# The fixed order of TensorE's work in a hybrid backbone's first mixer, set anew

## The chip, the cores and the metric

The kernel runs on one core of one Trainium2 chip, in one launch, with float32 inputs and output. The metric is device time in microseconds (us): the median of the runs shown. A profiled execution is taken beside them, from which the rows in this document come.

## What is computed

The program computes two layers of a diffusion backbone over 512 latent tokens and 256 context tokens, 1024 wide. The part that matters here is the mixer of layer 0. One input projection gives queries, keys, values and output gates of gated linear attention (GLA, 4 heads), a low-rank `z` from which its forget gates come, and queries, keys and values of ordinary attention:

```python
gq, gk, gv, gog, gz, aq, ak, av = _split(h @ w_in, EVEN_SIZES)
for d, z in enumerate(jnp.split(gz, 2, axis=-1)):
    logit = z @ gla_w_gate[d] + gla_b_gate[d]
    g = jax.nn.log_sigmoid(logit) / GLA_GATE_TAU
    # S_t = diag(exp(g_t)) S_{t-1} + k_t v_t^T,  o_t = S_t^T q_t, in both directions
```

The context is scanned alone, and the latent tokens start from its last state. Every sub-layer is also shifted, scaled and gated by vectors of a modulation, `silu(c) @ mod_w + mod_b`, for the latent tokens and for the context.

## The kernel before, in words

Tokens are kept in six tiles of 128 (0 to 3 latent, 4 and 5 context). A projection's float32 product is made of three matrix products of parts: weights and activations are split into a high and a low part (`wH`, `wL`), and `mm3` (L496) adds high by high, high by low and low by high. A weight unit is loaded by SyncE into `raw` (three buffers), cast by ScalarE to `wH` (L484), and what is left is put by VectorE into `wL` (L485); there are four buffers of each. "nat" products have tokens on the partitions and work two token tiles at a time in a two-bank PSUM tile (`mm_tile`, two buffers): 48 matmuls of 256 columns, called a block below. Queries and keys of GLA (`gqk`) come transposed, in groups of 512 and of 256 tokens. PSUM's eight banks are shared out as two two-bank tiles (`mm`), two single ones that `sc_tile` hands out in turn (`sc0`, `sc1`), and two of `tr_tile` (`tr`).

`even_mixer` (L825) first makes `z` (nat products of 288 columns), turns it (`zTp` to `zT`, L868 to L874) and then makes all of the forget factors in `gla_gates` (L982): for each of two head pairs, the context and the latent tokens, and two directions, one matmul gives `logit`, in bank `sc1` each time. ScalarE takes the absolute value, exponential, logarithm (L995 to L997), VectorE the minimum and the difference (L998, L999), ScalarE the last exponential into `glaf` (L1000).

After that, TensorE's order is written out by hand. Each word in the strings that `run` takes (L961 on) advances a generator by one step, and while `pinned` is set, TensorE's instructions stay in that program order. The other engines' order is chosen by a scheduler when the program is built, and is fixed from then on. The words are: `qk0`, `qk1` (GLA's queries and keys of a head pair), `v0`, `v1` (values), `g0`, `g1` (output gates), `q`, `kv` (ordinary attention's), `p` (its preparation, no matmuls), `m` (a step of the modulation), and `c0`, `l0`, `c1`, `l1`, the scans of head pair 0 and 1 over the context and the latent tokens.

A step `m` (`mod_vec`, L318) loads 512 KB of `mod_w` into `mraw` (three buffers in the pool `gate`) and lets VectorE add it to two accumulators `macc` (L340, L342). After eight steps TensorE sums over the partitions (`mod_acc`), VectorE copies the rows (`modrows`, L279), TensorE turns them (`modT`), and, for one of the two modulations here, turns a gate row (`gcT`). Both modulations end before the pool `gate` is given back (`tp.release()`), and the pool of the scans is opened in its place.

A scan (`scan`, L659) has six steps: (1) multiply queries and keys by decays in levels of 1, 2, 4 tokens, each level copied by ScalarE (`qkg`, L733) and then multiplied by VectorE (L738); (2) small score products of these levels (`pcg`, 32 by 32, into `sc` banks), and the levels 8 to 64; (3) `pcg` of the levels 8 and 16; (4) `pbg`, the scores of 32 and 64, and the keys turned (`knpg`, `tr` banks), which ScalarE copies (`kng`, L785); (5) the chunk states' products (`pdg`, in an `sc` bank, L794), and the chain of states on VectorE (`Sg`, L803, L805); (6) the outputs (`pog`, `tr` banks). The masked parts of `pcg` are taken out of the bank by ScalarE and VectorE (`CTg`, L717, L720).

## Time and profile before

| what | value |
|---|---|
| median of 3 runs | 1807.64 us (1806.29 to 1809.88) |
| the profiled execution's own time | 1812.69 us |
| its span, first to last instruction | 1810.8 us |
| mean granted TensorE clock | 0.975 |
| the mixer's `z` products end, attention's first transposes begin | 58.5 us, 293.0 us |

In rows of the timeline the columns are start, duration, engine, line, operation, output <- inputs, shape, count, and in brackets the idle time before and what ended it. In rows of a window table they are the stretch, its length, the busy time of TensorE, its weight loads, VectorE, ScalarE and GpSimd with counts, the granted TensorE clock (1.00 is full), and the DMA share and rate; a table for one tile has fewer columns. In grouped rows the count is followed by the busy time, the mean of one in ns, and the idle time before with its causes.

### The profile page before, as it was taken

The page shows a single profiled execution, that of the slowest core. Times are in us where ns is not written, and L with a number is a line of the kernel's source. Part 1 is how long each engine was busy: PE and PEld are TensorE (multiplying, and loading weights), DVE is VectorE, ACT ScalarE, POOL GpSimd, SP SyncE. Part 2 cuts the span into 40 slices and gives each one's busy share as a digit, 9 for nine tenths or more (in the row PEclk, how much of TensorE's full clock was granted, in tenths as well). Part 3 has the DMA queues.
Part 4 walks back from the last instruction along what each step waited for, and adds up shares of the span by engine and source line. Part 5 has one row for each costly group of instructions (what it writes and reads, how often), then busy time and mean ns, then how long its engine had stood idle before and what let it go on. Part 6 is the DMA issues. An engine that isn't in the chain of part 4 may idle for free. (4 is left out here: it accounts for less than half of the span.)

```text
span 1810.8 us, 33217 instructions
## 1 busy us (share of the span) xinstructions
PE 1728.3 (95%) x13864; PEld 1547.5 (85%) x13864; DVE 1299.4 (72%) x2095; ACT 877.4 (48%) x1562; POOL 59.1 (3%) x73
## 2 busy tenths in 40 slices
PE   6699888999999999999999999999999999999998
PEld 4488886787898888989899898888998899999997
DVE  5855485875596999888667715778875487878875
ACT  5526464764644333323334825666564464434442
POOL 1001020000000000000000100000000000000000
PEclk8699888999999999999999999999999999999999
DMA  8632103004433546454124412211114333333333
GB/s 312 189 100 59 42 21 102 21 2 151 140 111 87 152 144 195 149 165 139 58 63 149 140 47 71 60 48 53 55 48 129 110 100 99 111 94 94 94 106 127
DMA packets 169587, 187.28 MB, mean 103 GB/s; under 512 B 6198, under 2 KB 140892, under 8 KB 169436
## 3 DMA queue, kind: packets, MB, share of 16 engines
q1 hardware_dynamic: 167504, 181.56, 32.3%
q10 hardware_dynamic: 1932, 3.59, 0.6%
q8 instruction: 109, 1.79, 0.4%
q14 instruction: 42, 0.34, 0.1%
HBM read 175.66 MB, written 9.46 MB: 102 GB/s over the span
## 5 line engine op out<-in xcount | busy, mean ns | idle before, releaser
L485 DVE TENSOR_TENSOR wL<-raw,wH 128x1024 fp32r<-128x1024 f32 (+1 forms) x126 | 151.4, 1208 | 134.8 <-ACT wH L484 134.5
L165 PE MATMUL nat<-wH,x 128*128 128x256 f32 (+1 forms) x1216 | 230.5, 289 | 0.5 <-issue 0.5
L539 ACT CAST wH<-raw 128x1024 fp32r<-128x1024 f32 x120 | 124.6, 1052 | 177.7 <-PE acc L165 102.8
L165 PEld LDWEIGHTS nat<-wH,x 128*128 128x128 f32 x1216 | 195.1, 195 | 2.2 <-issue 1.1
L484 ACT CAST wH<-raw 128x1024 fp32r<-128x1024 f32 (+1 forms) x126 | 128.9, 1038 | 131.4 <-PE nat L165 37.9
L540 DVE TENSOR_TENSOR wL<-raw,wH 128x1024 fp32r<-128x1024 f32 x120 | 145.3, 1221 | 63.0 <-ACT wH L539 62.8
L165 PE MATMUL nat<-wL,x 128*128 128x256 f32 (+1 forms) x608 | 174.6, 287 | 0.0
L165 PE MATMUL acc<-wH,gH 128*128 128x512 f32 x440 | 172.6, 393 | 0.0
L165 PE MATMUL acc<-wH,gL 128*128 128x512 f32 x440 | 171.7, 390 | 0.0
L165 PE MATMUL acc<-wL,gH 128*128 128x512 f32 x440 | 171.5, 390 | 0.0
L632 DVE TENSOR_TENSOR y<-y,acc 128x1024 f32<-128x1024 f32 x135 | 114.8, 862 | 30.6 <-PE acc L165 27.3
L165 PE MATMUL ff<-x,wH 128*128 128x512 f32 (+1 forms) x512 | 127.6, 340 | 0.0
L342 DVE SCALAR_TENSOR_TENSOR macc<-mraw,scT,macc 128x1024 f32<-128x1024 f32 x98 | 122.9, 1279 | 6.3 <-DMA mraw<-in_mod_w_dram 6.2
L165 PEld LDWEIGHTS nat<-wL,x 128*128 128x128 f32 x608 | 118.6, 195 | 0.2 <-DVE wL L485 0.2
L412 POOL TENSOR_TENSOR rs<-ms,neghalf 128x1 f32<-128x1 f32 (+2 forms) x62 | 57.1, 923 | 1734.5 <-DVE ms L410 1734.5
L165 PE MATMUL oproj<-wH,x 128*128 128x512 f32 x320 | 102.8, 398 | 3.1 <-ACT x L453 3.0
L165 PEld LDWEIGHTS acc<-wH,gH 128*128 128x128 f32 x440 | 82.6, 188 | 19.8 <-issue 2.5
L165 PEld LDWEIGHTS acc<-wH,gL 128*128 128x128 f32 x440 | 82.6, 188 | 17.4
L165 PEld LDWEIGHTS acc<-wL,gH 128*128 128x128 f32 x440 | 82.7, 188 | 16.1
L165 PEld LDWEIGHTS ff<-x,wH 128*128 128x128 f32 x512 | 87.3, 190 | 10.0
L733 ACT COPY qkh<-arr 128x512 f32<-128x512 f32 x112 | 70.2, 642 | 36.3 <-DVE arr L738 32.1
L165 PE MATMUL ff<-x,wL 128*128 128x256 f32 (+1 forms) x256 | 86.2, 337 | 0.0
(329 smaller groups left out, 4134.4 us busy)
## 6 DMA issues: line engine op xcount, KB each, us to landing
mraw<-in_mod_w_dram SPq DMA_DIRECT2D x96, 512.0 KB, 4.5
raw<-in_ffn_w_gate_dram SPq DMA_DIRECT2D x44, 512.0 KB, 4.1
raw<-in_ffn_w_up_dram SPq DMA_DIRECT2D x44, 512.0 KB, 4.0
raw<-in_ffn_w_down_dram SPq DMA_DIRECT2D x44, 512.0 KB, 3.6
raw<-in_odd_w_in_dram SPq DMA_DIRECT2D x40, 512.0 KB, 4.6
raw<-in_even_w_in_dram SPq DMA_DIRECT2D x16, 512.0 KB, 3.6
x<-xr SPq DMA_DIRECT2D x14, 512.0 KB, 3.6
xr<-x SPq DMA_DIRECT2D x14, 512.0 KB, 3.5
```

The costliest lines, as they stand in the source:

```text
L165: return self.pin(self.nc.tensor.matmul(*a, **k))
L342: nc.vector.scalar_tensor_tensor(a, u, w, a, op0=ALU.mult, op1=ALU.add)
L412: nc.gpsimd.tensor_tensor(rs, ms, self.neghalf.to_broadcast([P, w]), op=ALU.pow)
L484: nc.scalar.copy(H[:, :m], raw[:, :m])
L485: nc.vector.tensor_tensor(L[:, :m], raw[:, :m], H[:, :m].bitcast(F32), op=ALU.subtract)
L539: self.nc.scalar.copy(H, f)
L540: self.nc.vector.tensor_tensor(L, f, H.bitcast(F32), op=ALU.subtract)
L632: nc.vector.tensor_tensor(y, y, pt, op=ALU.add)
L733: nc.scalar.copy(qkv[:, :, :, half, :], dst)
```

## The change

Four things. `gla_gates` becomes a generator that yields after each decay, and together with the turning of `z` it is the new word `e`; the eight `logit` products take the two `sc` banks in turn. The order strings are new: the first product of `qk0` now comes before `e`, and the decays stand in pairs between products. The words `m` and `e` are placed so that the modulation's last step comes after `tp.release()` (what it still does needs no tile of that pool). In a GLA scan the states' products `pdg` take `tr` banks instead of `sc` banks. The amount of arithmetic is the same.

```diff
-            pd = self.sc_tile(f"pd{nm}{d}").rearrange("p (s v) -> p s v", s=4)
+            pd = (self.tr_tile if hpp > 1 else self.sc_tile)(f"pd{nm}{d}").rearrange("p (s v) -> p s v", s=4)
...
-        fs = [self.gla_gates(mixg, tp, c, zT, wg) for c in range(2)]
+        fs = [[], []]
+
+        def decays():
+            for g in range(0, NTT, 4):
+                pt = self.tr_tile("zTp")
...
+            yield
+            for c in range(2):
+                yield from self.gla_gates(mixg, tp, c, zT, wg, fs[c])
...
-        run("qk0 qk0 m m m v0 qk0 m m qk0 m m qk0 m m q v0 m m m v0 m m m v0 m m m kv q m m m q m m m q m m m qk1 kv m m m kv m m m")
-        for _ in mods:
-            pass
+        run("qk0 qk0 e m qk0 e e v0 qk0 e e m qk0 e e m v0 e e m m q v0 m m v0 m m kv q m m q m q m m m m m m m m m qk1 kv m")
         tp.release()
...
-                pt = self.sc_tile(f"logit{c}{d}", 1)[:, :N]
+                pt = self.sc_tile(f"logit{c}{d}")[:, :N]
...
+                if d:
+                    fs.append(f)
+                yield
```

What this does to the engines' order is seen at three places. The first is TensorE behind the `z` products. Before, it turns `z` and makes the eight logits, and only then the first `gqk` product (x are the activations' parts):

```order
L168 MATMUL zTp<-ident,zn 32x128 x6
L165 MATMUL logit_636<-zT,wg 128x256
L165 MATMUL logit_645<-zT,wg 128x256
L165 MATMUL logit_655<-zT,wg 128x512
L165 MATMUL logit_664<-zT,wg 128x512
L165 MATMUL logit_675<-zT,wg 128x256
L165 MATMUL logit_684<-zT,wg 128x256
L165 MATMUL logit_694<-zT,wg 128x512
L165 MATMUL logit_703<-zT,wg 128x512
L165 MATMUL gqk_740<-x_311,wH 128x512
```

In the changed program the turning follows the first group of 24 `gqk` matmuls:

```order
L165 MATMUL gqk_652<-x_313,wL 128x512
L168 MATMUL zTp<-ident,zn 32x128 x6
L165 MATMUL gqk_652<-x_311,wH 128x256
...
L165 MATMUL gqk_652<-x_313,wL 128x256
L165 MATMUL logit_723<-zT,wg 128x256
L165 MATMUL logit_732<-zT,wg 128x256
L165 MATMUL gqk_753<-x_311,wH 128x512
...
L165 MATMUL gqk_753<-x_313,wL 128x512
L165 MATMUL logit_779<-zT,wg 128x512
L165 MATMUL logit_788<-zT,wg 128x512
```

The logits now stand in pairs, with 24 `gqk` matmuls between the first three pairs; the fourth pair stands behind the first block of `v0`.

The second place is VectorE at the end of the modulation's accumulations. Before, four accumulations in a row are followed by the copy of the first modulation's rows (the last weight split `wL` among them is that of `q`'s second half):

```order
L342 SCALAR_TENSOR_TENSOR macc_974<-mraw_1096,scT,macc_974 128x1024
L485 TENSOR_TENSOR wL<-raw,wH 128x1024
L342 SCALAR_TENSOR_TENSOR macc_975<-mraw_1096,scT,macc_975 128x1024
L342 SCALAR_TENSOR_TENSOR macc_974<-mraw_1100,scT,macc_974 128x1024
L342 SCALAR_TENSOR_TENSOR macc_975<-mraw_1100,scT,macc_975 128x1024
L279 COPY modrows<-mod_acc 128x512
```

In the changed program two splits, those of `kv`, stand there:

```order
L342 SCALAR_TENSOR_TENSOR macc_1187<-mraw_1254,scT,macc_1187 128x1024
L485 TENSOR_TENSOR wL<-raw,wH 128x1024 x2
L342 SCALAR_TENSOR_TENSOR macc_1186<-mraw_1258,scT,macc_1186 128x1024
L342 SCALAR_TENSOR_TENSOR macc_1187<-mraw_1258,scT,macc_1187 128x1024
L342 SCALAR_TENSOR_TENSOR macc_1186<-mraw_1262,scT,macc_1186 128x1024
L342 SCALAR_TENSOR_TENSOR macc_1187<-mraw_1262,scT,macc_1187 128x1024
L279 COPY modrows<-mod_acc 128x512
```

The copy still comes behind every accumulation of both modulations; on TensorE, the product `mod_acc` that it copies now follows four blocks (the three of `v0` and the first of `q`) instead of one.

The third place is SyncE's queue of loads. Before, once the first four `raw` loads behind the sixth `mraw` are through, eight `mraw` loads follow, of which these are the last two:

```order
L271 DMA mraw_1038<-in_mod_w_dram 128x1024
L271 DMA mraw_1092<-in_mod_w_dram 128x1024
L483 DMA raw<-in_even_w_in_dram 128x4x256
L271 DMA mraw_1096<-in_mod_w_dram 128x1024
L271 DMA mraw_1100<-in_mod_w_dram 128x1024
L483 DMA raw<-in_even_w_in_dram 128x8x128 x2
```

In the changed program `qk1`'s first weight load stands ahead of the last five:

```order
L271 DMA mraw_1242<-in_mod_w_dram 128x1024
L483 DMA raw<-in_even_w_in_dram 128x8x128
L271 DMA mraw_1246<-in_mod_w_dram 128x1024
L271 DMA mraw_1250<-in_mod_w_dram 128x1024
L271 DMA mraw_1254<-in_mod_w_dram 128x1024
L271 DMA mraw_1258<-in_mod_w_dram 128x1024
L271 DMA mraw_1262<-in_mod_w_dram 128x1024
L483 DMA raw<-in_even_w_in_dram 128x8x128
```

So five `mraw` loads wait in the queue until that load has found a free `raw` buffer.

In the scans, blocks stand in other gaps. Before, the second step of `l0` follows directly on `knpg` of `c0`; in the changed program a `gqk` group stands between, and `l0`'s second step follows `pdg`. The second steps of `l0`, `c1` and `l1` all follow directly on a `pdg` there, and the fourth and fifth step of `l1` follow each other with nothing between, as before. From the last output product of the mixer on, every engine's order is the same.

More of the change, by code (lines that the diff above doesn't have):

```diff
@@ L868, in even_mixer @@
             nc.scalar.dma_start(out=wg[16 * d : 16 * d + 16, d, :], in_=I["gla_w_gate"][0, d])
-        for g in range(0, NTT, 4):
-            pt = self.tr_tile("zTp")
-            n = min(4, NTT - g)
-            for i in range(n):
-                self.tr(pt[0:32, i * P : (i + 1) * P], zn[:, g + i, :], self.ident)
-            nc.vector.tensor_copy(zT[:, g * P : (g + n) * P], pt[0:32, : n * P])
-        fs = [self.gla_gates(mixg, tp, c, zT, wg) for c in range(2)]
+        fs = [[], []]
+        def decays():
+            for g in range(0, NTT, 4):
+                pt = self.tr_tile("zTp")
+                n = min(4, NTT - g)
+                for i in range(n):
+                    self.tr(pt[0:32, i * P : (i + 1) * P], zn[:, g + i, :], self.ident)
+                nc.vector.tensor_copy(zT[:, g * P : (g + n) * P], pt[0:32, : n * P])
+            yield
+            for c in range(2):
+                yield from self.gla_gates(mixg, tp, c, zT, wg, fs[c])
         self.lower_bounds()
@@ L949, in even_mixer @@
             "c0": lambda: job(0, 0), "l0": lambda: job(0, 1), "c1": lambda: job(1, 0), "l1": lambda: job(1, 1),
-            "r0": lambda: (readout(0, (t,)) for t in tiles),
+            "e": decays, "r0": lambda: (readout(0, (t,)) for t in tiles),
         }
@@ L960, in even_mixer @@
         self.pinned = True
-        run("qk0 qk0 m m m v0 qk0 m m qk0 m m qk0 m m q v0 m m m v0 m m m v0 m m m kv q m m m q m m m q m m m qk1 kv m m m kv m m m")
-        for _ in mods:
-            pass
+        run("qk0 qk0 e m qk0 e e v0 qk0 e e m qk0 e e m v0 e e m m q v0 m m v0 m m kv q m m q m q m m m m m m m m m qk1 kv m")
         tp.release()
         gp = self.open_pool("gla")
-        run("c0 l0 kv c0 v1 qk1 c0 qk1 qk1 c0 l0 qk1 c0 c1 v1 c0 l0 g0 v1 l0 p v1 l0 c1 p p g0 l0 c1 l1 g1 p g0 c1 p g0 c1 l1 p p")
-        run("g1 c1 l1 g1 l1 l1 r0 r0 r0 g1 l1")
+        run("c0 l0 kv m c0 kv c0 v1 qk1 c0 qk1 c0 l0 qk1 c0 g0 qk1 l0 c1 v1 l0 v1 l0 c1 p v1 l0 c1 l1 p g1 g0 c1 p g0 c1 l1 p g0 c1 p p")
+        run("g1 l1 p g1 l1 l1 r0 r0 r0 g1 l1")
         gp.release()
@@ L980, in even_mixer, with gla_gates @@
         return cat
-    def gla_gates(self, mixg, tp, c, zT, wg):
+    def gla_gates(self, mixg, tp, c, zT, wg, fs):
         nc = self.nc
         self.tc.keep_in_program_order(nc.scalar.preload_act_table_set("natural_log_exp_and_others"))
-        fs = []
         for t0, N in ((SEQ, CTX), (0, SEQ)):
@@ L1000, in gla_gates @@
                 nc.scalar.activation(f[:, d, :], m, AF.Exp, scale=1.0 / 16.0)
-            fs.append(f)
-        return fs
+                if d:
+                    fs.append(f)
+                yield
     def gla_job(self, gp, c, t0, nt, f, gq, gk, gv, first, ends):
```

## Prediction

> **What bounds the kernel now.** The page comes first.

> ```profile
> span 1810.8 us, 33217 instructions
> PE 1728.3 (95%) x13864; PEld 1547.5 (85%) x13864; DVE 1299.4 (72%) x2095; ACT 877.4 (48%) x1562; POOL 59.1 (3%) x73
> ...
> PEclk8699888999999999999999999999999999999999
> ```

> TensorE carries the whole, and its clock is below full only in the first eighth of the span, which holds the mixer. The change moves nothing outside it, so only the mixer's holes count. The first is the stretch from the end of the `z` products to the first `v0` block, in the windows; behind it is the group of logits in that stretch.

> ```profile
> 58.53:104.67 46.14, 32.50 (x120) 20.62 (x118) 40.18 (x48) 21.93 (x39) 0.00 (x0) 0.70 0.58 176
> L165 PE MATMUL logit<-zT,wg 32*128 32x256 f32 (+1 forms) x16 | 12.4, 875 | 13.3 <-DVE am L998 11.8 <-issue 1.5
> ```

> TensorE waits 13.3 us there for VectorE to empty the one logit bank, and the clock falls to 0.70 in the mean. The second kind of hole is in the scans, in TensorE's waits from 160 to 293 us (who waited for whom, total, times, longest):

> ```profile
> PE pcg L165 <- DVE Sg L805: 6.0, 3, 3.9
> PE pcg L165 <- issue: 5.9, 3, 2.9
> PE pcg L165 <- ACT qkg L733: 1.2, 1, 1.2
> PE pcg L165 <- DVE CTg L720: 1.1, 1, 1.1
> PE pdg L165 <- ACT kng L785: 0.6, 2, 0.3
> ```

> That is 14.8 us. Behind it comes the clock, in windows:

> ```profile
> 169.00:172.50 3.50, 1.65 (x70) 1.53 (x71) 2.96 (x13) 3.50 (x15) 0.00 (x0) 1.00 0.50 150
> 172.50:176.00 3.50, 3.50 (x19) 3.50 (x19) 1.86 (x9) 1.81 (x8) 0.00 (x0) 0.51 0.02 5
> 182.80:186.20 3.40, 2.10 (x170) 1.81 (x171) 1.34 (x5) 2.63 (x8) 0.00 (x0) 1.00 0.02 5
> 186.20:193.00 6.80, 6.37 (x113) 6.30 (x113) 4.10 (x10) 3.15 (x6) 0.00 (x0) 0.50 0.02 5
> ```

> A stretch in which TensorE is busy for 1.65 of 3.5 us, or 2.10 of 3.4 with tiny matmuls, is followed by half clock.

> **The decays between products.** The price of the work itself, from the timeline and from the windows of the tile `gqk` (two groups each in the first two rows, one in the third):

> ```profile
> 58.53 0.60 PE L168 MATMUL zTp<-ident,zn 128*32 128x128 f32 x4
> 59.43 0.39 PE L168 MATMUL zTp<-ident,zn 128*32 128x128 f32 x2 [0.31 <-ACT zn L858]
> 61.37 0.67 PE L165 MATMUL logit<-zT,wg 32*128 32x256 f32 x2 [1.54 <-issue]
> 66.66 2.07 PE L165 MATMUL logit<-zT,wg 32*128 32x512 f32 x2 [2.49 <-DVE am L998]
> ...
> 96.33:104.84 8.51, 8.51 (x50) 1.00 0.59 180
> 171.70:181.90 10.20, 10.09 (x48) 8.79 (x48) 0.00 (x0) 0.00 (x0) 0.83 0.21 61
> 187.90:193.40 5.50, 5.34 (x24) 5.14 (x24) 0.00 (x0) 0.00 (x0) 0.53 0.01 3
> ```

> Four `gqk` groups at full clock are 2 x 8.5 = 17.0 us; the turning is 1.0; four narrow logits are 4 x 0.67. A wide one was seen at half clock alone, 2.07: at full clock it is between 1.04 (it scales) and 2.07; I take 1.04, since the narrow one does scale (0.67). That makes 17.0 + 1.0 + 2.7 + 4.2 = 24.9 us in place of 46.1. Waits that are new: each pair of logits needs both banks emptied by VectorE, whose order puts two or three accumulations ahead; a `gqk` group or a block lies between, so I expect 1.0 us in sum, and at most 2.5 at each of three pairs (the longest wait now). The gain is 46.1 - 24.9 - 1.0 = 20.2 us. ScalarE's one more table load is covered: it is busy for 21.93 of those 46.14 us.

> **VectorE's accumulations.** They hid behind the logits' holes; now TensorE comes to `modT`, which needs `modrows`, while they still run. VectorE's prices, from its groups between 57.9 and 111 us and from its timeline, and the two waits that stand there now:

> ```profile
> L342 DVE SCALAR_TENSOR_TENSOR macc<-mraw,scT,macc 128x1024 f32<-128x1024 f32 x25 | 31.1, 1278 | 0.0
> L485 DVE TENSOR_TENSOR wL<-raw,wH 128x1024 fp32r<-128x1024 f32 x6 | 7.3, 1222 | 2.9 <-ACT wH L484 2.9
> L998 DVE TENSOR_SCALAR am<-logit,col 128x256 f32<-128x256 f32 (+1 forms) x8 | 4.9, 616 | 3.1 <-ACT am L995 2.9
> L999 DVE TENSOR_TENSOR am<-am 128x256 f32<-128x256 f32 (+1 forms) x8 | 4.4, 551 | 0.0
> L340 DVE TENSOR_SCALAR macc<-mraw,scT 128x1024 f32<-128x1024 f32 x2 | 1.4, 746 | 0.0
> L874 DVE COPY zT<-zTp 32x512 f32<-32x512 f32 (+1 forms) x2 | 1.0, 537 | 0.0
> ...
> 98.64 7.26 DVE L342 SCALAR_TENSOR_TENSOR macc<-mraw,scT,macc 128x1024 f32<-128x1024 f32 x6
> ...
> 112.40 0.66 PE L168 MATMUL modT<-ident,modrows 128*128 128x128 f32 x4 [0.81 <-DVE modrows L279]
> 113.69 0.27 PE L168 MATMUL gcT<-ident,gc 128*16 128x128 f32 x1 [0.63 <-DVE gc L388]
> ```

> From 57.9 us on, the changed order has 24 accumulations to the copy of `modrows` (7.26 / 6 = 1.21 each: 29.0), eight weight splits (9.8), the decays' 16 operations (9.3), the first two products of the second modulation (1.4) and `zT` (1.0): 50.5 us, so VectorE ends at 108.4 if it never idles. TensorE comes to `mod_acc` at 58.5 + 24.9 + 1.0 + 4 blocks x 6.02 (row below) = 108.5. They meet. `kv`'s two splits, ahead of the last four accumulations, wait for casts into buffers that `v0`'s last block frees at about 102.5, so I expect VectorE some 1 us late: 1.6 us of wait with the copy, against 0.81 + 0.63 now. The term is -0.2 (from +1.4 to -5, the latter if VectorE idles 6 us).

> **The scans.** With `pdg` in the `tr` banks, the `sc` banks that `pcg` needs are empty as soon as ScalarE has copied `pbg`: the 6.0 us behind `Sg` go. The `tr` banks are free in time: `pdg` waits for `kng` anyway, and `pog` for `Sg`. The levels are late next; blocks in the gaps give them time, and I leave 0.7 of the 2.3 us of `qkg` and `CTg`, and the 0.6 of `kng`, as `l1`'s fourth and fifth step still stand together. The waits called issue:

> ```profile
> 186.63 1.44 PE L165 MATMUL pcg<-qkg 64*32 64x32 f32 x90 [1.74 <-issue]
> ...
> 225.32 0.32 PE L165 MATMUL pcg<-qkg 64*32 64x32 f32 x3 [2.89 <-issue]
> ...
> 260.49 1.06 PE L165 MATMUL pcg<-qkg 64*32 64x32 f32 x58 [1.32 <-issue]
> ...
> q8 instruction: 109, 1.79, 0.4%
> ```

> They fall inside runs of `pcg`, the shortest instructions; the instruction queue brings 1.79 MB in 109 packets, 16.4 KB each. The long runs of `l0` and `l1` stay whole, so I keep 1.74 and 1.32, and half of 2.89: 4.5 of 5.9 us. Gain: 6.0 + 1.6 + 1.4 = 9.0 us.

> [...]

> **The clock in the scans.** Blocks at half clock, in the windows of the tile `nat`:

> ```profile
> 203.00:209.10 6.10, 6.02 (x48) 5.81 (x48) 0.00 (x0) 1.00 0.02 5
> 225.50:233.80 8.30, 8.20 (x48) 7.99 (x48) 0.00 (x0) 0.69 0.01 2
> 261.40:268.95 7.55, 7.42 (x48) 7.21 (x48) 0.02 (x1) 0.78 0.01 2
> ```

> They lose 2.2 and 1.4 us, the `gqk` groups 10.09 - 8.5 = 1.6 and 5.34 - 2.8 (a third of 8.5) = 2.5: 7.7. With a block in most gaps I expect two such stretches to stay, behind the long runs of `l0` and `l1`, at 2.2: 4.4. Gain 3.3.

> [...]

> **Sum.** 20.2 - 0.2 + 9.0 + 3.3 = 32.3 us. Something comes off for the order of ScalarE and VectorE, which is fixed and puts attention's preparation among the levels. Now it holds up a level once in this way, by a scaling that waits for GpSimd's `rs`:

> ```profile
> 165.29 0.83 ACT L1073 ACTIVATE natq<-natq,rs 128x64 f32<-128x64 f32 x3 [3.75 <-POOL rs L412]
> ```

> With TensorE sooner there, such a stall has less cover; I put one on the path, 3.7 us. That leaves 28.6. The profiled execution's 1812.69 becomes 1784.1; the median lies 5.05 below the profiled one, so the forecast is **1779.0 us**.

> **Rivals.**

> *Issue takes the bank waits' place.* The 6.0 us come back, and the half clock with them (3.3): a gain of 19.3, 1788. For: the issue waits stand in the very runs that `Sg` held up. Against: the one at 186.63 follows no bank wait. Chance 0.2.

> *ScalarE's order is the next bound.* For: the row above. Against: its 21.93 us of 46.14 leave room. Three such stalls on the path instead of one, and the half clock behind them (3.3), are 10.8 us more: a gain of 17.8, 1790. Chance 0.12.

> *Nothing new comes.* No such stall (3.7), no wait at `modT` (1.6), and issue and half clock at half (4.5): a gain of 38.4, 1769. Chance 0.1.

> *SyncE starves the accumulations: slower than before.* `qk1`'s first load stands ahead of five `mraw` loads and waits for a `raw` buffer that the split of `q`'s second half frees, which waits for the weight buffer that the fourth `gqk` group gives back, at X. Then come a cast and a split (2.4 us if the cast takes as long), a load to its landing (4.1, below), and ten accumulations (12.1), with two splits (2.4) between.

> ```profile
> mraw<-in_mod_w_dram SPq DMA_DIRECT2D x16, 512.0 KB, 4.1
> ```

> The wait at `modT` begins once X + 21 is over 108.5, so from X = 88, and grows with X; at X = 117 the 28.6 us are gone. I expect X at 58.5 + 17.0 + 1.0 + 3.4 for two pairs of logits = 80; now that group ends at 104.8. Chance 0.03.

> *The change does nothing*, since some hole moves elsewhere in full: 1807.6, chance 0.02.

> **How the numbers follow.** The forecast's own case, a gain of 23 to 34, has 0.53. The range reaches down to 1768.5, the case without new waits, and up to 1791, which takes in both costly rivals and, of the bounds, wide logits at 2.07 (4.1) together with 5 at `modT`. A measurement here tells about 0.2% (3.6 us) from no change. Faster has 0.53 + 0.2 + 0.12 + 0.1 = 0.95, slower 0.03, the same 0.02.

> **What would show it.** Right: no `logit` wait over 1 us and full clock to about 108 us; `modT` behind `modrows` for 1 to 2 us; no `pcg` behind `Sg`; and attention's first `kT` 28.6 us sooner, at about 264, than it is now:

> ```profile
> 293.02 0.44 PE L168 MATMUL kT<-ident,natk 128*128 128x128 f32 x2 [0.67 <-ACT gvo L1021]
> ```

> Wrong: `pcg` behind issue for over 8 us (first rival), `pcg` or `pdg` behind ScalarE for over 8 (second), or `modT` waiting for over 10 (fourth).

## The result, and the profile after

The changed kernel takes 1778.55 us (median of 4 runs, 1777.81 to 1780.20), the kernel before on the same chip 1808.76 (4 runs, 1806.29 to 1811.83): a ratio of 0.9833, 95% interval 0.9816 to 0.9851. The forecast was 1779.0.

The page of the changed kernel, span, TensorE's share and its clock:

```profile
span 1777.0 us, 33231 instructions
PE 1714.8 (96%) x13864; PEld 1540.1 (87%) x13864; DVE 1297.1 (73%) x2095; ACT 876.9 (49%) x1563; POOL 57.2 (3%) x73
...
PEclk8998998999999999999999999999999999999999
```

The clock's first dip stands ahead of the `z` products as before (0.50 from 29.0 to 39.2 us; before, from 25.8 to 39.4). The long one behind it (0.50 from 63.3 to 90.6 us before) is gone. The stretch from the end of the `z` products to the second block of `v0`, and a stretch in the scans to which I come back, in the windows:

```profile
58.62:89.76 31.14, 29.98 (x168) 23.58 (x166) 29.29 (x38) 20.30 (x36) 0.00 (x0) 1.00 0.71 220
155.20:165.40 10.20, 8.93 (x280) 7.55 (x281) 6.90 (x19) 9.38 (x28) 0.00 (x0) 0.50 0.18 55
```

The first holds all that the 46.14 us held before, and one block of 6.02 us more: 25.1 us for the same work, at a granted clock of 1.00 in place of 0.70. VectorE is busy for 29.29 of the 31.14 us: it now works beside TensorE where TensorE used to wait for it. Who waited for whom on TensorE from 56 to 262 us (total, times, longest):

```profile
PE pdg L165 <- ACT kng L785: 3.7, 5, 2.2
PE pcg L165 <- issue: 3.1, 2, 2.0
PE modT L168 <- DVE modrows L279: 1.5, 1, 1.5
PE logit L165 <- issue: 1.2, 1, 1.2
```

No `logit` waits for VectorE any more, `modT` waits 1.5 us behind all accumulations, and no `pcg` waits behind `Sg`. New is `pdg` behind `kng`, 3.7 us for 0.6. Two rows of TensorE's timeline cut the mixer into the part up to the second `modT` and the part behind it; first of the changed kernel, then the one of before that the prediction did not show:

```profile
128.85 0.60 PE L168 MATMUL modT<-ident,modrows 128*128 128x128 f32 x4
260.19 0.44 PE L168 MATMUL kT<-ident,natk 128*128 128x128 f32 x2 [0.67 <-ACT gvo L1023]
```

```profile
138.01 0.60 PE L168 MATMUL modT<-ident,modrows 128*128 128x128 f32 x4
```

At the second `modT` the changed kernel is 9.2 us ahead and has done two blocks more (12.0 us): 21.2 us. At the first `kT` of attention it is 293.02 - 260.19 = 32.8 us ahead, so the scans brought 11.6. Behind that `kT` the two profiled executions differ by 1.0 us (1517.8 and 1516.8 to the end of the span). Medians and ratios below leave out single runs far above the others of their kernel (4286, 5029, 7438 and 1794.55 us), of which the last is a profiled execution, at a mean clock of 0.913 for 0.98 to 0.99 in the others, so no time is read from that profile.

### The profile page after: what moved, and what is told of

It reads as the page before. It is cut to its first block, busy times and chain, and to the rows that moved or that the text cites. A ratio compares the mean times of both kernels' runs of the same rounds, so it can differ in the third digit from the quotient of the medians.

```text
span 1777.0 us, 33231 instructions
## 1 busy us (share of the span) xinstructions
PE 1714.8 (96%) x13864; PEld 1540.1 (87%) x13864; DVE 1297.1 (73%) x2095; ACT 876.9 (49%) x1563; POOL 57.2 (3%) x73
## 3 DMA queue, kind: packets, MB, share of 16 engines
q8 instruction: 109, 1.79, 0.4%
## 5 line engine op out<-in xcount | busy, mean ns | idle before, releaser
L485 DVE TENSOR_TENSOR wL<-raw,wH 128x1024 fp32r<-128x1024 f32 (+1 forms) x126 | 151.3, 1207 | 120.8 <-ACT wH L484 120.4
L165 PE MATMUL nat<-wH,x 128*128 128x256 f32 (+1 forms) x1216 | 229.0, 287 | 0.0
L165 PEld LDWEIGHTS nat<-wH,x 128*128 128x128 f32 x1216 | 193.5, 193 | 3.0 <-ACT natq L894 0.8
L484 ACT CAST wH<-raw 128x1024 fp32r<-128x1024 f32 (+1 forms) x126 | 128.9, 1038 | 123.1 <-PE nat L165 39.3
L165 PE MATMUL nat<-wL,x 128*128 128x256 f32 (+1 forms) x608 | 173.7, 286 | 0.4 <-issue 0.3
L165 PE MATMUL acc<-wH,gH 128*128 128x512 f32 x440 | 172.6, 393 | 0.0
L165 PE MATMUL acc<-wH,gL 128*128 128x512 f32 x440 | 171.7, 390 | 0.0
L165 PE MATMUL acc<-wL,gH 128*128 128x512 f32 x440 | 171.5, 390 | 0.0
L165 PE MATMUL ff<-x,wH 128*128 128x512 f32 (+1 forms) x512 | 127.6, 340 | 0.0
L342 DVE SCALAR_TENSOR_TENSOR macc<-mraw,scT,macc 128x1024 f32<-128x1024 f32 x98 | 122.7, 1278 | 5.0 <-DMA mraw<-in_mod_w_dram 5.0
L165 PEld LDWEIGHTS nat<-wL,x 128*128 128x128 f32 x608 | 117.4, 193 | 0.3 <-DVE wL L485 0.3
L412 POOL TENSOR_TENSOR rs<-ms,neghalf 128x1 f32<-128x1 f32 (+2 forms) x62 | 55.4, 895 | 1704.7 <-DVE ms L410 1649.8
L165 PE MATMUL oproj<-wH,x 128*128 128x512 f32 x320 | 103.4, 401 | 3.0 <-ACT x L453 2.8
L165 PEld LDWEIGHTS acc<-wH,gH 128*128 128x128 f32 x440 | 82.6, 188 | 19.8 <-issue 2.5
L165 PEld LDWEIGHTS acc<-wH,gL 128*128 128x128 f32 x440 | 82.6, 188 | 17.4
L165 PEld LDWEIGHTS acc<-wL,gH 128*128 128x128 f32 x440 | 82.7, 188 | 16.1
L165 PEld LDWEIGHTS ff<-x,wH 128*128 128x128 f32 x512 | 87.3, 190 | 10.1
L733 ACT COPY qkh<-arr 128x512 f32<-128x512 f32 x112 | 70.0, 643 | 36.5 <-DVE arr L738 32.2
L165 PE MATMUL ff<-x,wL 128*128 128x256 f32 (+1 forms) x256 | 86.2, 337 | 0.0
## 6 DMA issues: line engine op xcount, KB each, us to landing
mraw<-in_mod_w_dram SPq DMA_DIRECT2D x96, 512.0 KB, 4.4
raw<-in_ffn_w_gate_dram SPq DMA_DIRECT2D x44, 512.0 KB, 4.1
raw<-in_ffn_w_up_dram SPq DMA_DIRECT2D x44, 512.0 KB, 3.9
raw<-in_ffn_w_down_dram SPq DMA_DIRECT2D x44, 512.0 KB, 3.7
raw<-in_odd_w_in_dram SPq DMA_DIRECT2D x40, 512.0 KB, 4.5
raw<-in_even_w_in_dram SPq DMA_DIRECT2D x16, 512.0 KB, 4.3
x<-xr SPq DMA_DIRECT2D x14, 512.0 KB, 3.6
xr<-x SPq DMA_DIRECT2D x14, 512.0 KB, 3.3
```

Of the source, the lines that this page charges most:

```text
L165: return self.pin(self.nc.tensor.matmul(*a, **k))
L342: nc.vector.scalar_tensor_tensor(a, u, w, a, op0=ALU.mult, op1=ALU.add)
L412: nc.gpsimd.tensor_tensor(rs, ms, self.neghalf.to_broadcast([P, w]), op=ALU.pow)
L484: nc.scalar.copy(H[:, :m], raw[:, :m])
L485: nc.vector.tensor_tensor(L[:, :m], raw[:, :m], H[:, :m].bitcast(F32), op=ALU.subtract)
L733: nc.scalar.copy(qkv[:, :, :, half, :], dst)
```

## The experiments

All ratios are against runs of the kernel before on the same chip.

| kernel | median us | ratio to before, 95% interval | first `kT` at |
|---|---|---|---|
| `pdg` in `tr` banks alone | 1796.88 | 0.9926 (0.9913 to 0.9939) | 281.14 |
| new first string alone | 1784.82 | 0.9861 (0.9846 to 0.9876) | 268.84 |
| new first string and `pdg` in `tr` | 1775.81 | 0.9814 (0.9794 to 0.9834) | 257.81 |
| changed, `pdg` in `sc` | 1782.84 | 0.9851 (0.9832 to 0.9869) | 266.33 |
| changed, one logit bank | 1800.14 | 0.9955 (0.9942 to 0.9968) | 280.92 |
| before, two logit banks alone | 1801.62 | 0.9970 (0.9957 to 0.9983) | 284.92 |
| changed, pool given back late | 1782.51 | 0.9852 (0.9835 to 0.9868) | 260.61 |
| changed, `pcg` ahead of `pdg` | 1780.07 | 0.9843 (0.9830 to 0.9855) | 263.88 |
| the same, runs in halves | 1774.60 | 0.9806 (0.9786 to 0.9825) | 253.84 |
| old places, runs in halves | 1777.95 | 0.9832 (0.9811 to 0.9852) | 261.19 |
| the same, 32 matmuls more | 1771.07 | 0.9797 (0.9781 to 0.9812) | not read |
| changed, hole filled | 1778.19 | 0.9837 (0.9824 to 0.9850) | 260.93 |

Two things bear on the last column. The profiled executions of "new first string and `pdg` in `tr`" (1771.84) and of "the same, runs in halves" (1766.76) are the fastest runs of their kernels, 4.0 and 7.8 us below the medians. And up to the second `modT` the changed kernel and the eight below that keep its first string and two logit banks (the last but one aside) do the same work: it stands at 128.2 to 129.1 us in six of them, but at 129.9 with `pcg` ahead of `pdg`, at 130.1 with the hole filled, and at 131.2 with the old places in halves. Those 1.0, 1.3 and 2.3 us more than the changed kernel's 128.85 are no cost of the edits to the scans.

### Which part pays in the scans

Four kernels take the change apart. `pd_alone` is the kernel before with this edit, and `new_order_old_banks` the changed kernel without it:

```diff
-            pd = self.sc_tile(f"pd{nm}{d}").rearrange("p (s v) -> p s v", s=4)
+            pd = (self.tr_tile if hpp > 1 else self.sc_tile)(f"pd{nm}{d}").rearrange("p (s v) -> p s v", s=4)
```

`first_string_and_pd` is the changed kernel with the scans' strings of before, fitted to the first string (one step `m` and one of `kv` are done there now); `first_string_alone` is the same with `pdg` in `sc` banks:

```diff
-        run("c0 l0 kv m c0 kv c0 v1 qk1 c0 qk1 c0 l0 qk1 c0 g0 qk1 l0 c1 v1 l0 ...
+        run("c0 l0 kv m kv c0 v1 qk1 c0 qk1 qk1 c0 l0 qk1 c0 c1 v1 c0 l0 g0 v1 ...
-        run("g1 l1 p g1 l1 l1 r0 r0 r0 g1 l1")
+        run("g1 c1 l1 g1 l1 l1 r0 r0 r0 g1 l1")
```

> The kernel before with one part of the change alone: pdg takes the tr banks. First theory (the terms of the sum add up): the three waits of pcg behind Sg go (6.0 us), and with the longest of them the half clock behind it (1.4 us); between 4.5 and 8 us less than before, so 1801 to 1804 us, and no row of pcg behind Sg. Rival (issue takes the place of the bank waits): pcg behind issue rises from 5.9 to over 9 us, and the gain is under 3 us: 1806 to 1809.

> The changed kernel with the scans' strings and the banks of pdg of before, so that only the decays between products, the two logit banks and the modulation's new places stay. First theory: TensorE comes to the second modT 21 us sooner at equal work, and all of that arrives at the end: 1786 to 1790 us. Rival (the levels on ScalarE and VectorE were hidden behind the late start and are late next): part of it is given back as waits of pcg, pbg or pdg in the scans, and the time is over 1793.

> The changed kernel with the scans' strings of before: decays between products and pdg in tr banks, old places of the blocks in the scans. First theory: the gains of the two parts add, 21 and 4.5 to 8 us: 1779 to 1785 us, so that the new places of the blocks are worth 0 to 6 us. Rival (the blocks' new places are what pays in the scans): over 1785.

> The changed kernel with pdg back in the sc banks; TensorE's order is the same as in the changed kernel. First theory: three pcg runs follow directly on pdg there as before, so waits behind Sg of some 6 us come back and the half clock behind the longest with them: 1783 to 1788 us. Rival (issue and the scalings for kng stand in the same places and hide the bank waits): within 2 us of the changed kernel's 1778.6.

Of `pdg` alone, TensorE's waits in the scans:

```profile
PE pcg L165 <- issue: 5.2, 3, 2.2
PE pcg L165 <- ACT qkg L733: 1.2, 1, 1.2
PE pcg L165 <- DVE CTg L720: 1.1, 1, 1.1
```

Its windows around the two places where `Sg` held `pcg` up longest before, and then the same two places of the kernel before:

```profile
216.40:226.30 9.90, 8.98 (x203) 8.62 (x203) 9.85 (x32) 5.08 (x11) 0.00 (x0) 1.00 0.40 110
243.90:257.10 13.20, 11.13 (x324) 10.82 (x324) 12.84 (x36) 10.74 (x27) 1.17 (x2) 0.87 0.01 2
```

```profile
217.40:233.80 16.40, 11.46 (x203) 10.99 (x203) 13.73 (x41) 5.53 (x11) 0.00 (x0) 0.79 0.22 66
251.30:268.95 17.65, 12.42 (x323) 11.99 (x323) 16.37 (x42) 9.74 (x23) 4.17 (x3) 0.71 0.11 32
```

The row behind `Sg` is gone, and issue did not take its place (5.2 for 5.9). The two stretches, with the same 203 and some 323 matmuls, shrink by 6.5 and 4.5 us, while only 2.0 and 3.9 us of the wait lay in them: the rest is issue (2.89 to 0.92 at the first, though 1.32 to 2.07 at the second) and the clock, 0.79 to 1.00 and 0.71 to 0.87. At the first `kT` it is 11.9 us, in the medians 12.5. So my first theory had the mechanism and too small a size (4.5 to 8 us); here the waits cost their own length and what followed them, issue and a lowered clock (0.79 and 0.71 in these stretches).

The first string alone came 24.2 us sooner to `kT` (expected 21 or a little less): 21.2 up to the second `modT` and 3.0 in the scans. Both together: 35.2, nearly the sum (36.1). Both medians lie below what was expected (1784.82 for 1786 to 1790, 1775.81 for 1779 to 1785). That leaves less than nothing for the new places of the blocks: the changed kernel's `kT` is 2.4 us later than that of the kernel with the old places. With `pdg` in `sc` banks the new places were 2.5 us ahead (268.84 and 266.33); the waits behind `Sg` came back there as expected (7.6 us for some 6), and the time is 1782.84 for 1783 to 1788. In the medians both differences (2.7 and 2.0 us) lie within overlapping intervals, so the places are worth nothing that these runs can tell. What they do is trade waits. The kernel with the old places has these, the changed one those shown above:

```profile
PE pcg L165 <- issue: 6.3, 3, 3.3
...
PE pdg L165 <- ACT kng L785: 0.6, 2, 0.3
```

The 2.3 us behind `qkg` and `CTg` are gone with the old places too, once the first string is new, so my term for them (1.6) was no gain of the places. The new ones cut issue from 6.3 to 3.1 and pay 3.1 behind `kng`. Why `kng` is late there stands in ScalarE's timeline of the changed kernel:

```profile
152.92 1.30 ACT L1075 ACTIVATE natq<-natq,rs 128x64 f32<-128x64 f32 x5 [4.14 <-POOL rs L412]
154.13 0.35 ACT L770 COPY STg<-pbg 128x256 f32<-128x256 f32 x1
154.38 0.35 ACT L1075 ACTIVATE natq<-natq,rs 128x64 f32<-128x64 f32 x1
154.63 0.35 ACT L770 COPY STg<-pbg 128x256 f32<-128x256 f32 x1
154.88 0.37 ACT L785 COPY kng<-knpg 128x256 f32<-128x256 f32 x1
```

A scaling for attention's preparation stands ahead of the copies in ScalarE's fixed order and waits 4.14 us for GpSimd. That is the stall I had put on the path; TensorE waits 2.2 us for it, with the half clock of the window 155.20:165.40 behind.

### Two banks or gaps between the logits

`one_logit_bank` is the changed kernel with one edit, `two_banks_alone` the kernel before with the reverse one:

```diff
-                pt = self.sc_tile(f"logit{c}{d}")[:, :N]
+                pt = self.sc_tile(f"logit{c}{d}", 1)[:, :N]
```

> The changed kernel with all logits in one bank again, TensorE's order unchanged. First theory: the second logit of each of the four pairs waits for VectorE as the seven did before (11.8 us over seven, 1.7 us each), 7 us in sum; 1.5 us of that only take the place of the wait at modT, where TensorE then comes later: 5 to 6 us slower than the changed kernel, 1783 to 1786. Rival (the gap alone does it, two banks add nothing): within 2 us of 1778.6.

> The kernel before with one edit: the eight logits take the two sc banks in turn, with nothing between them on TensorE, as before. First theory (banks and places are each worth little alone, since with one bank the changed order lost 23 us again): the pairs still wait for VectorE, some 3 us at three pairs and a half clock behind them, so the gain is 2 to 7 us: 1801 to 1807. Rival (the second bank alone is what pays): 1784 to 1792, as the changed first string gave without the change in the scans.

With one bank and the changed order, the wait of `logit`, the window of the decays, and the second `modT` in the timeline:

```profile
PE logit L165 <- DVE am L999: 11.5, 4, 4.4
```

```profile
59.89:111.00 51.11, 39.04 (x172) 29.54 (x171) 44.44 (x51) 24.39 (x41) 0.00 (x0) 0.80 0.55 174
```

```profile
150.37 0.60 PE L168 MATMUL modT<-ident,modrows 128*128 128x128 f32 x4
```

The expectation of 5 to 6 us fell: it costs 21.6 us, and the second `modT` is 21.5 us later than in the changed kernel. The order between products has then gained nothing in this stretch, since 150.37 less two blocks is 138.3, against 138.01 before. Four waits take as long as seven did (11.5 and 11.8), because VectorE's order now has more ahead of the reading of the bank, here from the first pair:

```profile
69.30 2.46 DVE L342 SCALAR_TENSOR_TENSOR macc<-mraw,scT,macc 128x1024 f32<-128x1024 f32 x2
71.69 1.21 DVE L485 TENSOR_TENSOR wL<-raw,wH 128x1024 fp32r<-128x1024 f32 x1
72.82 1.27 DVE L342 SCALAR_TENSOR_TENSOR macc<-mraw,scT,macc 128x1024 f32<-128x1024 f32 x1
74.02 0.47 DVE L999 TENSOR_SCALAR am<-logit,col 128x256 f32<-128x256 f32 x1
```

A mean wait of before (1.7 us) was the wrong price for another order, and the lost clock (0.80 in place of 1.00) was not in my expectation at all. Two banks in the old order, the wait of `logit` and the second `modT`:

```profile
PE logit L165 <- DVE am L998: 5.0, 3, 2.8
```

```profile
132.55 0.60 PE L168 MATMUL modT<-ident,modrows 128*128 128x128 f32 x4
```

Here the second `modT` comes 5.5 us sooner than before and the first `kT` 8.1; in the medians it is 5.8 us, as expected (2 to 7). So in this stretch the gaps alone bring nothing, the banks alone 5.5, and both together 21.2: pairs with a bank each leave TensorE no wait, and full gaps give VectorE the time to empty them.

### The pool given back sooner

The last step of the modulation goes back ahead of the release, behind the same blocks:

```diff
-        run("... m m qk1 kv m")
+        run("... m m qk1 kv m kv m"); [None for _ in mods]
...
-        run("c0 l0 kv m c0 kv c0 v1 qk1 ...
+        run("c0 l0 c0 kv c0 v1 qk1 ...
```

> The changed kernel with the modulation's last step put back ahead of the release of its pool, behind the same blocks of TensorE. First theory: nothing changes, within 2 us of 1778.6, since the scans' first levels have to wait for mod_acc either way, which frees the tiles. Rival: the first scan's levels begin behind the second modT, some 6 us later, and pcg of the first scan waits for 3 to 6 us: 1781 to 1785.

In the timeline:

```profile
260.61 0.44 PE L168 MATMUL kT<-ident,natk 128*128 128x128 f32 x2 [0.67 <-ACT gvo L1023]
```

The first `kT` moves by 0.4 us, and no wait appears in the first scan. The median is 4 us higher with an interval that overlaps the changed kernel's; since the trace has no such time in the mixer, I take this part of the change as worth nothing, without having shown the 4 us to be noise.

### Waits that trade places

Two swaps of words, and then a cut of the two long runs of small matmuls into halves (`compact` yields between its two heads, for the latent tokens' first levels):

```diff
-... qk1 c0 l0 qk1 c0 g0 ... g0 c1 l1 p g0 c1 p p
+... qk1 l0 c0 qk1 c0 g0 ... g0 l1 c1 p g0 c1 p p
```

```diff
-... qk1 c0 l0 qk1 c0 g0 ... g0 c1 l1 p g0 c1 p p
+... qk1 l0 c0 qk1 l0 c0 g0 ... g0 l1 c1 p g0 l1 c1 p p
```

> The changed kernel with two swaps: the second step of l0 ahead of the fifth of c0, and the second step of l1 ahead of the fifth of c1, so that a run of pcg stands between knpg and pdg. First theory: pdg's waits for kng there (2.2 and 0.9 us) go, and with the first of them the half clock behind it; the waits called issue stay, since the run of pcg is as long as before: 3 to 8 us less than the changed kernel, 1770.5 to 1775.5. Rival (the waits behind ScalarE and issue trade places): issue rises by as much, within 2 us of 1778.6.

> As the swapped kernel, and the second step of l0 and of l1 is cut in two, one half of 128 small matmuls ahead of pdg and one behind the next block, so that no run of small matmuls is longer than 152. First theory: issue comes from a run of over some 250 instructions that are shorter than their own supply, so its 3.1 us go too, and with them the last half clock in the scans: 8 to 12 us less than the changed kernel, 1766.5 to 1770.5. Rival (issue comes wherever a packet of instructions ends inside small matmuls, whatever the length of the run): issue stays at 2 us or more and the time is within 2 us of the swapped kernel's.

The swapped kernel's waits from 128 to 262 us:

```profile
PE pcg L165 <- issue: 4.9, 2, 2.6
PE pcg L165 <- ACT STg L770: 1.6, 2, 1.4
PE pdg L165 <- ACT sq L940: 1.1, 1, 1.1
PE pdg L165 <- ACT kng L785: 0.6, 2, 0.3
```

My theory fell: the 3.1 us behind `kng` went, and 2.7 us behind other work of ScalarE and 1.8 us of issue came. The first `kT` is 3.7 us later, 2.7 of it in the scans, and the time is not 3 to 8 us less but within 2 us, the rival's case. The waits of the kernel in halves:

```profile
PE pcg L165 <- DVE CTg L720: 2.0, 1, 2.0
...
PE pcg L165 <- ACT STg L770: 1.6, 2, 1.4
```

Issue is gone, and the first `kT` is 6.4 us sooner than in the changed kernel and 10.0 sooner than in the swapped one, in the fastest of its runs. The expected 8 to 12 us were not reached: 2.0 us behind `CTg` are new. The median is only 4 us below the changed kernel's, over runs from 1766.76 to 1777.24; what differs between those runs is open.

### What issue is

The halves put into the old places, and then the same with 32 matmuls that only repeat others:

```diff
-... qk1 c0 l0 qk1 c0 c1 v1 ... g0 c1 p g0 c1 l1 p p
+... qk1 c0 l0 qk1 c0 l0 c1 v1 ... g0 c1 l1 p g0 c1 l1 p p
```

```diff
-                        for j in range(4):
+                        for j in (0, 1, 2, 3) * (2 if nm == "g04" and hh == 0 and levels[0][2] is not None else 1):
```

> The kernel of the decays between products and pdg in tr banks with the scans' strings of before (1775.8 us), and in addition the second step of l0 and of l1 in halves of 128 small matmuls: the first directly on knpg, the second directly on pdg, a block between. First theory: the 5.4 us of issue in the two long runs go, and the half clock behind them, 2 to 4 us: 6 to 10 us less, 1766 to 1770. Rival (what goes as issue comes back as waits for CTg or STg, which the halves need sooner): within 3 us of 1775.8.

> The kernel with the old places and the halves (1777.95 us), and 32 small matmuls more: the first head's pcg of levels 8 and 16 of the first scan is made twice, to the same values. That moves every later instruction of TensorE by 32. First theory (issue comes where the end of a packet of instructions falls behind a stretch of some 127 matmuls that are nearly all small, at a fixed count of instructions): the ends of the packets fall 32 matmuls earlier in the runs, with longer matmuls in the stretch before, so the two issue waits (2.4 and 0.9 us) go or fall below 0.6, and with the first the half clock behind it (1.5 us): attention's first kT some 4 us sooner than 261.2 though there is 0.35 us more work, 1773 to 1775. Rival (issue comes from the length of a run of small matmuls): issue stays within 1 us of 3.3, and the time is the same or higher by 0.4.

In the old places the halves did not help: 1777.95 against 1775.81, the rival's case, and 130.0 us from the second `modT` to `kT` against 129.4. One issue wait stands behind 127 of the 128 small matmuls of a half, with the last alone behind it, in the timeline:

```profile
166.19 0.46 PE L165 MATMUL pcg<-gqk,gqk 64*32 64x32 f32 x32
166.47 1.05 PE L165 MATMUL pcg<-qkg 64*32 64x32 f32 x95
169.94 0.21 PE L165 MATMUL pcg<-qkg 64*32 64x32 f32 x1 [2.42 <-issue]
```

In its waits, one for `STg` has come too, as the rival had it:

```profile
PE pcg L165 <- issue: 3.3, 2, 2.4
PE pcg L165 <- ACT STg L770: 2.7, 1, 2.7
```

So the length of a run is not what decides. With 32 matmuls more ahead of them, both issue waits left the runs of `pcg`; one of 0.9 us shows inside a `gqk` group instead. Of these waits only the places are read:

```profile
PE pcg L165 <- ACT STg L770: 2.8, 1, 2.8
PE gqk L165 <- issue: 0.9, 1, 0.9
```

The median fell to 1771.07, 6.9 us less for more work (the intervals of the two ratios just touch). That is the first theory's case, and by more than its 3 to 5 us; how much more, these runs do not tell.

### The hole filled

Sixteen matmuls of 256 columns behind the second `gqk` group of the second head pair, into a part of the bank that nothing reads; on the other engines one cast of ScalarE comes six places later:

```diff
-                    self.gemm_T(pt, Ws[x], h, (g,))
+                    self.gemm_T(pt, Ws[x], h, (g,)); [self.mm(pt[:, NT : NT + 256], Ws[x][0][:, 0, :], h.hl(0, slice(0, 256))[0], start=True, stop=True) for _ in range(16 if x == 1 and g is groups[-1] else 0)]
```

> The changed kernel with 16 more matmuls of 256 columns behind the second gqk group of the second head pair, into a part of its bank that nothing reads: some 2 us of work that changes no result, in the place where TensorE waits for kng (2.2 us). First theory (the clock is halved behind a stretch of some 3.4 us in which TensorE is busy for under two thirds or so, and not by a wait as such): with the hole filled the clock stays full from 155 to 165 us; pdg, pcg and the next group take 3.5 us less there, up to 0.6 us comes back as issue: attention's first kT 3 to 3.5 us sooner than 260.2 in spite of more work, about 1775. Rival (the clock follows the kind of work, small matmuls, and not the hole): half clock stays, and the time is within 1 us of 1778.6.

The stretch in pieces of 3.4 us, first of the changed kernel, then with the hole filled:

```profile
151.80:155.20 3.40, 1.30 (x11) 1.09 (x10) 0.18 (x1) 2.28 (x10) 3.00 (x2) 1.00 0.00 1
155.20:158.60 3.40, 3.30 (x116) 2.80 (x120) 1.19 (x5) 3.34 (x13) 0.00 (x0) 0.51 0.02 5
158.60:162.00 3.40, 2.23 (x172) 2.10 (x163) 2.41 (x5) 3.40 (x11) 0.00 (x0) 0.50 0.09 11
```

```profile
151.80:155.20 3.40, 3.40 (x31) 3.40 (x30) 0.42 (x3) 1.04 (x5) 3.02 (x2) 1.00 0.18 62
155.20:158.60 3.40, 2.91 (x92) 2.30 (x93) 1.37 (x5) 3.34 (x14) 0.84 (x1) 1.00 0.00 0
158.60:162.00 3.40, 1.51 (x178) 1.40 (x168) 0.17 (x1) 3.40 (x13) 0.00 (x0) 1.00 0.02 5
162.50:165.90 3.40, 3.40 (x9) 2.71 (x9) 3.33 (x11) 2.45 (x6) 0.00 (x0) 0.50 0.45 133
```

And the waits called issue in its scans:

```profile
PE pcg L165 <- issue: 4.2, 2, 2.4
```

The clock part held: with TensorE busy over 151.8 to 155.2, the next two pieces run at full clock. The size did not: the faster run of `pcg` met its issue wait earlier and it grew (4.2 us in sum for 3.1), a piece with 1.51 of 3.4 us busy resulted, and the half clock came behind that one. The first `kT` is at 260.93, the median 1778.19: no gain. From the second `modT` on it is 0.5 us sooner than in the changed kernel (130.8 and 131.3 us), not 3 to 3.5.

## Why the prediction was right, and where only by chance

**Decays.** 24.9 us of work and 1.0 of waits were predicted, 25.1 came; the term was 20.2 and was 21.0. What I had not seen is how it hangs on both edits at once, since either alone gives 0 or 5.5 us. Two readings were wrong without moving the sum: of the 13.3 us of waits, 11.8 were for VectorE and 1.5 were issue, of which 1.2 stay; and the clock of before is under 0.9 in slices up to the seventh of forty, so beyond the first eighth.

**`modT`.** TensorE was to meet VectorE there with a wait of 1.6 us; it is 1.5. SyncE's later loads, the rival that ended slower, did not show.

**Scans.** The terms were 9.0 and 3.3, less one stall of 3.7: 8.6 us. 11.6 came, and not from where I put it. The step that failed is the sharing out: I gave the banks their 6.0 us of wait and the places of the blocks most of the rest (1.6 for `qkg` and `CTg`, 1.4 of issue, two stretches of half clock). The banks alone bring 11.9, issue and clock with them, and the places between +2.5 and -2.4 us, by the banks they meet. From the second `modT` to `kT`, at equal work, the 11.6 are, rounded, 3.0 of the new first string, 10.6 of the banks behind it, and -1.9 of the places.

**The stall.** One scaling behind GpSimd's `rs` on the path, as predicted, for 3.7 us: TensorE waits 2.2 us there, of 3.1 more behind `kng` in all, with 10.2 us of half clock behind it. The hole filled shows that this half clock hangs on the idle time there.

**Rivals.** Issue did not take the bank waits' place: it is 5.2 us with the banks alone and 3.1 in the changed kernel. A little of it did come: with the new places it is 1.8 us with `pdg` in `sc` banks and 3.1 in `tr`. ScalarE's order is a bound at one place, not at three. Nor did nothing new come: the mixer's 32.8 us lie nearer to the forecast's 28.6 than to the 38.4 of that case.

**The median.** The sum was 4.2 us short in the mixer and 1.0 behind it. I had also carried over the 5.05 us by which the profiled execution of before lay above its median; the changed kernel's profiled execution lies 0.3 above its own (1778.82 and 1778.55). 4.2 + 1.0 - 4.8 is the 0.4 us by which the forecast missed. That it is so small is chance: these are two errors of some 5 us each.

No version here beats the changed kernel by much. The best is the last but one, with the halves in the old places and 32 useless matmuls, at 0.9797 of before (0.9781 to 0.9812) against 0.9833 (0.9816 to 0.9851).

## What to carry to other kernels

Price a wait with the clock behind it: here the clock fell to 0.50 or 0.51 behind pieces of 3.4 us in which TensorE was busy for 1.30, 1.51 and 2.10 us (it stayed at 1.00 behind one with 1.88), and with this and issue the bank waits cost 11.9 us in place of 6.0. A second bank and work between the products that use it can each be worth little and together much (here 5.5 us, nothing, and 21.2 together), so test them together. And a profiled execution's distance to the median is its own: compare trace with trace and median with median, and don't carry one over to the other.

## What the runs showed of the hardware

The clock fell behind pieces with 1.30 and 1.51 of 3.4 us busy (to 0.51 and 0.50) and stayed at 1.00 behind one with 2.91, as the windows above show. The busy share alone does not decide: around the changed kernel's wait at `modT` (107.50 to 110.90 us) TensorE is busy for 1.88 of 3.40 us, and the clock stays at 1.00 behind it, as it does behind 2.25 of 3.40 among its decays (66.50 to 69.90); in the kernel before, 2.10 of 3.40 (182.80 to 186.20) were followed by 0.50. What else decides is open. In the case with 1.51 the longest single idle time was 1.88 us.
